# The second half's output weights converted behind the mixing operands of the first prefill blocks, in a hybrid attention and mLSTM step

## The chip, the cores and the metric

The kernel runs on one core of one Trainium2 chip. The metric is the device time of one execution in microseconds. The five engines are named as in the profile: PE (TensorE), DVE (VectorE), ACT (ScalarE), POOL (GpSimd) and SP (SyncE, which here only issues transfers).

## The reference

One layer of a diffusion backbone. An attention head group (8 query heads, 2 key heads, width 64) and a bidirectional mLSTM group (4 heads, width 128) read one input projection side by side; one output projection merges them, and a SwiGLU network follows. There are 128 context rows and 1024 latent rows of width 1024, in float32. The part that matters here:

```python
attn_o = attention(aq, keys, vals)
hm, st_f, st_b = mlstm_bidir(heads(mq), heads(mk) * (MLSTM_DK ** -0.5), heads(mv), gates, init_f, init_b)
hm = (hm.reshape(B, T, MLSTM_WIDTH) * jax.nn.sigmoid(mo)).astype(x.dtype)
mix = jnp.concatenate([attn_o, hm], axis=-1) @ w_out
x = x + g1 * mix
h2 = rmsnorm(x, norm2_w) * (1 + sc2) + sh2
x = x + g2 * swiglu(h2, w_gu, w_down)
```

## The kernel before

The rows are cut into nine blocks of 128 (block 0 is the context), and three blocks make a chunk. Every large product is done three times, so as to keep float32 precision: a matrix is split into a rounded part and the rest of it, and high by high, low by high and high by low are added in the same accumulator. So each weight piece, once loaded (`raw`, L162), is rounded by ACT (`whi`, L163) and its rest is taken by DVE (`wlo`, L141). A product of one row block with half of the output columns is 12 matmuls: four each on L1219, L1221 and L1223.

The order of work is not written out by hand. Python generators for the parts of the program are woven into each other, and a scheduler that keeps its own timeline then orders the instructions of each engine. `tc.issue_after(x)` and `behind(key)` put a floor under that: what is made inside stands behind instruction x, where it runs on x's engine. Every engine then runs its own list strictly in order. Memory comes from pools; a tile has a tag, and with `bufs=1` the next tile of the tag waits until the readers of the one before are done. A pool that opens later can lie on the memory of one that is closed.

The change is in the stretch from about 480 to 590 us, where the mLSTM scan ends and the output projection takes over. `attn_out_first` (L1320) has done the attention half of it for the first three blocks, using the tiles `gta` and `mxa` of the pool hTp; its parts `ada` make the gate rows of the last modulation, two half rows of 512, each one with a bias row from b_ada (L477), a product (L479), a sum (L480), a scaling (L482), and a store to the scratch tensor g_d by ACT's queue (L483). `prefill` (L1226) then does the mLSTM half for all nine blocks:

- `mix(b)` transposes a block's mLSTM rows `hmr` on PE (L120); ACT rounds them into the tile `mx` (L1265), DVE takes the rest (L141).
- `half(b, n)` is the 12 matmuls of block b with column half n; DVE multiplies by the gate (L1180, into a tile t2), POOL adds to the row (L1181).
- `end(b)` squares and sums a finished row on ACT (`jk`, L1398), with the reciprocal root on DVE (L131 to L137), and runs `norm2`: ACT scales the rows to `y` (L1414), PE transposes them, ACT and DVE shift them (`fl`, L1422 and L1424), and so the SwiGLU network gets its operands.

`out_pieces(1, n)` loads and splits the weights of the column half n for the mLSTM rows. Into all this the attention of the next chunk is woven: queries `qr` are loaded from q_d (L1078, ACT's queue), transposed (L120) and rounded (`qT`, L1089); then scores S (L1111), their maximum on DVE (L1113), exponentials on ACT (`pr`, `ph`), transposes by DMA on SP's queue (`phT`, `plT`), and the product with the values (`po`, L1135 and L1136).

Of the kernel before, what the change touches and what calls it, by code (L numbers as in the profile page):

```python
# [8 lines left out]
F32 = mybir.dt.float32  # L9
# [10 lines left out]
P = 128  # L20
# [26 lines left out]
def hybrid_step(ctx: ExitStack, tc: tile.TileContext, I: dict, O: dict):  # L47
# [92 lines left out]
    def sub(out, full, hi, eng):  # L140
        (dve if eng == "dve" else pool).tensor_tensor(out=out, in0=full, in1=hi, op=ALU.subtract)  # L141

# [131 lines left out]
    es1 = ExitStack()  # L274
    hTp = es1.enter_context(tc.tile_pool(name="hTp", bufs=1, reuse_waits="tile"))
    gp = es1.enter_context(tc.tile_pool(name="gp", bufs=1, reuse_waits="tile"))
# [144 lines left out]
    hp = ctx.enter_context(tc.tile_pool(name="hpk", bufs=1, side="right", reuse_waits="tile"))  # L421
    hT = [(hTp if c < 2 else rowp).tile([P, 2, KD, CT], F16, name=f"hT{c}", tag=f"hT{c}" if c < 2 else "b4") for c in range(NCH)]
    hTh, hTl = [t[:, 0] for t in hT], [t[:, 1] for t in hT]
# [752 lines left out]

    def add_gated(x1, ps, g, n, eng=dve):
        cs = slice(n * 512, (n + 1) * 512)
        t = t2()
        dve.tensor_tensor(out=t, in0=ps, in1=g, op=ALU.mult)  # L1180
        eng.tensor_tensor(out=x1[:, cs], in0=x1[:, cs], in1=t, op=ALU.add)  # L1181
# [44 lines left out]
    def prefill(cur, nxt):  # L1226
# [4 lines left out]
        def load_hm(b):  # L1231
            if b >= NB:
                return None
            hm = xe.tile([P, 512], F32, name=nm("hmr"), tag="hmr", bufs=2)
            if b < CB:
                loaded["hm"] = dma(hm, hm_d[0][b * P : (b + 1) * P, :]).ins
            else:
                r = dma(hm.rearrange("p (h n) -> p h n", n=P), hm_d[b // CB][:, :, b % CB * P : (b % CB + 1) * P])
                if b == CB:
                    loaded["hm"] = r.ins  # L1240
            return hm
# [9 lines left out]
        gate = loaded["gate"] = dma(gx_all, g_d[0, 0:1, :].to_broadcast([P, D])).ins  # L1251
        ws.append(out_pieces(1, 1))
        cur["gate"] = loaded["piece"]
        gx = [gx_all[:, n * 512 : (n + 1) * 512] for n in range(2)]
        mixed = {}

        def mix(b):
            t = xe.tile([P, NQ, P], F32R, name=nm("mx"), tag="mx", bufs=3)
            th, tl = mixed[b] = t[:, 0:4], t[:, 4:8]
            hm = hms.pop(0)  # L1260
            ps = bank()
            for j in range(4):
                transpose(ps[:, j * P : (j + 1) * P], hm[:, j * P : (j + 1) * P])
            psv = ps.rearrange("p (j x) -> p j x", j=4)
            nc.scalar.copy(th, psv)  # L1265
            sub(tl, psv, th.bitcast(F32), "dve")
            with tc.issue_after(gate):
                hms.append(load_hm(b + 2))

        def half(b, n):  # L1270
# [29 lines left out]
        yield  # L1300
        yield from end(0)
        load_x1(3)
# [3 lines left out]
        yield  # L1306
        yield from end(1)
        for b in range(2, NB):
            load_x1(b + 2)
            half(b, 0)  # L1310
            yield
            if b + 1 < NB:
                mix(b + 1)
                yield
            half(b, 1)
            yield
            yield from end(b)

    def attn_out_first(oT, ready):


        x1 = rowp.tile([P, CB, D], F32, name="x1a", tag="b4")
        gt = hTp.tile([P, 6, 512], F32, name="gta", tag="hT1")
        mx = hTp.tile([P, CB, NQ, P], F32R, name="mxa", tag="hT0")
# [236 lines left out]
    for name, bufs in (("mm1", 1), ("po", 1)):  # L1561
        psum[name] = ctx.enter_context(tc.tile_pool(name="q" + name, bufs=bufs, space=PSUM, reuse_waits="tile"))
    homes["wq"] = ctx.enter_context(tc.tile_pool(name="wq", bufs=1, reuse_waits="tile"))
    xe = ctx.enter_context(tc.tile_pool(name="xe", bufs=1, reuse_waits="tile"))
    xg = ctx.enter_context(tc.tile_pool(name="xg", bufs=1, reuse_waits="tile"))
# [116 lines left out]
```

## Time and profile before

| | us |
|---|---|
| median of 3 runs | 1529.1 |
| the runs | 1527.36, 1529.1, 1534.01 |
| the profiled execution | 1531.07 |
| its span, first to last instruction | 1529.3 |
| PE busy | 1473.0 (96%) |
| DVE busy | 1015.8 (66%) |
| ACT busy | 770.4 (50%) |
| POOL busy | 268.8 (18%) |
| mean granted TensorE clock | 0.989 |

A row of the timeline has start, duration, engine, line, operation, output and inputs, shapes, the count of instructions taken together, and in brackets the idle time of the engine before it and what ended that. ACTq and SPq are the queues that issue transfers. Matmuls are pipelined, so a group's duration reaches over the start of the next.

### The profile page before, as it was taken

To read this page: it belongs to the slowest core of one execution; us is meant where nothing else is said; L and a number is where in the kernel's file an instruction comes from. 1 tells how busy PE (TensorE), PEld (TensorE's weight loads), DVE (VectorE), ACT (ScalarE), POOL (GpSimd) and SP (SyncE) were. 2 spreads that over 40 slices of the span, in tenths; PEclk is the share of its full clock that TensorE was granted. 3 is DMA by queue.
4 is the path that set the end of the run, shared out by engine and by line. 5 is a ranking of instruction groups with operands and counts; after the bars stand their busy time and mean duration, and the time that the engine had idled before them with its cause. 6 is when DMAs were issued, how large, how long until landed. Compare 5 with 4: busy or idle time off the path is not lost.

```text
span 1529.3 us, 23410 instructions
## 1 busy us (share of the span) xinstructions
PE 1473.0 (96%) x8539; PEld 1244.7 (81%) x8539; DVE 1015.8 (66%) x2025; ACT 770.4 (50%) x1429; POOL 268.8 (18%) x354
## 2 busy tenths in 40 slices
PE   6899999999998899999999999999999999999997
PEld 3545567677766789999898999989998989999996
DVE  4887654838568866878637587787866585554554
ACT  4764475947654645556433444656553443323333
POOL 0113423333344441010010100100010101101110
PEclk9899999999999999999999999999999999999998
DMA  9664323523456577869635357886864445544541
GB/s 359 205 198 147 101 71 42 120 53 62 110 177 207 135 180 187 200 156 195 171 115 166 124 184 212 198 184 145 201 145 138 138 139 179 158 135 126 153 144 56
DMA packets 387113, 233.77 MB, mean 153 GB/s; under 512 B 170102, under 2 KB 347462, under 8 KB 386998
## 3 DMA queue, kind: packets, MB, share of 16 engines
q1 hardware_dynamic: 385006, 228.69, 55.0%
q10 hardware_dynamic: 1864, 3.20, 0.9%
q8 instruction: 67, 1.10, 0.3%
q14 instruction: 48, 0.39, 0.1%
q0 software_dynamic: 128, 0.39, 0.1%
HBM read 182.21 MB, written 11.69 MB: 127 GB/s over the span
## 4 chain that ended last, share of the span: by engine, by line
PE 78%; DVE 5%; DMA 3%; ACT 3%; issue 1%; POOL 1%; SPq 0%; ACTq 0%; DVEq 0%; POOLq 0%
PE mm L1437 11%; PE mm L1436 11%; PE mm L1435 11%; PE mm L1191 5%; PE mm L1192 5%; PE mm L1193 5%; PE S L1111 4%; PE wi L514 3%; PE wi L513 3%; PE wi L512 3%; PE mm L1219 2%; PE po L1136 2%; PE po L1135 2%; PE mm L1221 2%; PE mm L1223 2%
## 5 line engine op out<-in xcount | busy, mean ns | idle before, releaser
L163 ACT CAST whi<-raw 128x1024 fp32r<-128x1024 f32 x214 | 219.2, 1026 | 367.8 <-PE mm L1436 146.9
L141 DVE TENSOR_TENSOR wlo<-raw,whi 128x1024 fp32r<-128x1024 f32 x214 | 257.7, 1204 | 170.5 <-ACT whi L163 167.0
L1436 PE MATMUL mm<-aTl,whi 128*128 128x384 f32 x1056 | 354.4, 336 | 0.0
L1437 PE MATMUL mm<-aTh,wlo 128*128 128x384 f32 x1056 | 354.2, 336 | 0.0
L1435 PE MATMUL mm<-aTh,whi 128*128 128x384 f32 x1056 | 353.2, 335 | 0.0
L141 POOL TENSOR_TENSOR hl<-tn,hl 128x384 fp32r<-128x384 f32 x66 | 84.9, 1286 | 846.6 <-ACT hl L1458 796.4
L1435 PEld LDWEIGHTS mm<-aTh,whi 128*128 128x128 f32 x1056 | 198.3, 188 | 0.7
L1436 PEld LDWEIGHTS mm<-aTl,whi 128*128 128x128 f32 x1056 | 198.3, 188 | 0.6
L1437 PEld LDWEIGHTS mm<-aTh,wlo 128*128 128x128 f32 x1056 | 198.3, 188 | 0.1
L1191 PE MATMUL mm<-whi,hl 128*128 128x512 f32 x372 | 144.4, 392 | 1.1 <-DVE t L1180 1.1
L1192 PE MATMUL mm<-wlo,hl 128*128 128x512 f32 x372 | 145.1, 391 | 0.0
L1193 PE MATMUL mm<-whi,hl 128*128 128x512 f32 x372 | 142.7, 391 | 0.0
L1118 DVE SCALAR_TENSOR_TENSOR pl<-pr,st,ph 128x1152 f16<-128x1152 f32 (+1 forms) x72 | 96.9, 1346 | 37.3 <-ACT ph L1117 35.9
L1113 DVE TENSOR_REDUCE st<-S 128x1 f32<-128x1152 f32 (+1 forms) x72 | 88.9, 1234 | 17.5 <-PE S L1111 17.2
L1114 ACT ACTIVATE pr<-S,st 128x1152 f32<-128x1152 f32 (+1 forms) x72 | 81.3, 1129 | 33.0 <-DVE st L1113 28.2
L1117 ACT ACTIVATE ph<-pr,st 128x1152 f16<-128x1152 f32 (+1 forms) x72 | 83.8, 1164 | 26.3 <-issue 10.9
L1180 DVE TENSOR_TENSOR t<-mm,gl 128x512 f32<-128x512 f32 x102 | 69.1, 686 | 38.1 <-PE mm L1193 16.0
L512 PE MATMUL wi<-headw,hT 128*128 128x384 f16 x288 | 93.9, 326 | 0.2 <-ACT th L799 0.2
L513 PE MATMUL wi<-headw,hT 128*128 128x384 f16 x288 | 93.9, 326 | 0.0
L514 PE MATMUL wi<-headw,hT 128*128 128x384 f16 x288 | 93.9, 326 | 0.0
L1111 PE MATMUL S<-kst,qT 128*128 128x384 f32 (+1 forms) x400 | 84.5, 344 | 0.8 <-ACT pr L1114 0.8
L1191 PEld LDWEIGHTS mm<-whi,hl 128*128 128x128 f32 x372 | 69.9, 188 | 15.2 <-DVE t L1180 1.5
(400 smaller groups left out, 2591.3 us busy)
## 6 DMA issues: line engine op xcount, KB each, us to landing
raw<-in_w_gu_dram SPq DMA_DIRECT2D x132, 512.0 KB
raw<-in_w_down_dram SPq DMA_DIRECT2D x60, 512.0 KB
a<-in_w_ada_dram SPq DMA_DIRECT2D x24, 512.0 KB
gl<-g_d SPq DMA_DIRECT2D x36, 256.0 KB
aw<-in_w_ada_dram SPq DMA_DIRECT2D x16, 512.0 KB
iraw<-in_w_in_dram SPq DMA_DIRECT2D x32, 256.0 KB
x<-in_x_sample_dram SPq DMA_DIRECT2D x11, 512.0 KB
raw<-in_w_out_dram SPq DMA_DIRECT2D x10, 512.0 KB
```

What stands on the lines that cost most here:

```text
L141: (dve if eng == "dve" else pool).tensor_tensor(out=out, in0=full, in1=hi, op=ALU.subtract)
L163: nc.scalar.copy(hi[:, :n], raw[:, :n])
L512: mm(ps[:, :n], ah, wh[:, k % 2, c0 : c0 + n], start=(k == 0), stop=False)
L513: mm(ps[:, :n], ah, wl[:, k % 2, c0 : c0 + n], start=False, stop=False)
L514: mm(ps[:, :n], al, wh[:, k % 2, c0 : c0 + n], start=False, stop=(k == KD - 1))
L1111: mm(S[:, n, 0:w], qT[:, h, :], kst[kv][:, t, c0 + n * w : c0 + (n + 1) * w], start=(t == 0), stop=(t == 1))
L1191: mm(ps, ah, wh[:, k % 2, :], start=(k == 0), stop=False)
L1192: mm(ps, ah, wl[:, k % 2, :], start=False, stop=False)
L1193: mm(ps, al, wh[:, k % 2, :], start=False, stop=(k == nk - 1))
L1435: mm(ps, wh[:, k, :], th[:, k, :], start=(k == 0), stop=False)
L1436: mm(ps, wh[:, k, :], tl[:, k, :], start=False, stop=False)
L1437: mm(ps, wl[:, k, :], th[:, k, :], start=False, stop=(k == KD - 1))
```

## The change

1. `out_pieces(1, 1)`, the second column half's weights, is made after `mix(0)` and `mix(1)`, with a floor: its rounding on ACT and its subtraction on DVE stand behind those of block 1's mixing operands. The first two blocks are mixed in one go.
2. The pool of `gta` and `mxa` is split in two, and `hmr` gets a pool of its own (xh, opened ahead of xe), so that the mixing tiles lie on other memory.
3. The loads of `hmr` for blocks 2 and 3 are issued behind the load of the gate rows, after the two mixes; `norm2` of a block comes one half later, behind `half(b + 3, 0)`.
4. The products with the gate of blocks 0 and 1 go into the attention's buffers "pr", not into the three t2 tiles.
5. The second bias row of the gate goes into the attention's tile "qr", not into `hmx`.

```diff
-    hTp = es1.enter_context(tc.tile_pool(name="hTp", bufs=1, reuse_waits="tile"))
+    hTp = [es1.enter_context(tc.tile_pool(name=f"hTp{c}", bufs=1, reuse_waits="tile")) for c in (1, 0)][::-1]
...
-            hm = xe.tile([P, 512], F32, name=nm("hmr"), tag="hmr", bufs=2)
+            hm = xh.tile([P, 512], F32, name=nm("hmr"), tag="hmr", bufs=2)
...
         gate = loaded["gate"] = dma(gx_all, g_d[0, 0:1, :].to_broadcast([P, D])).ins
-        ws.append(out_pieces(1, 1))
-        cur["gate"] = loaded["piece"]
...
-            nc.scalar.copy(th, psv)
-            sub(tl, psv, th.bitcast(F32), "dve")
-            with tc.issue_after(gate):
-                hms.append(load_hm(b + 2))
+            loaded["mx"] = nc.scalar.copy(th, psv).ins
+            loaded["ml"] = sub(tl, psv, th.bitcast(F32), "dve").ins
+            if b > 1:
+                with tc.issue_after(gate):
+                    hms.append(load_hm(b + 2))
...
-                add_gated(x1s[c][i], ps, g, n, pool)
+                if b < 2:
+                    if b == 0:
+                        mixed["t", n] = ap2.tile([P, 3, CT], F32, name=nm("t2"), tag="pr", bufs=2).rearrange("p a n -> p (a n)")
+                    t = mixed["t", n][:, b * 512 : (b + 1) * 512]
+                else:
+                    t = None
+                add_gated(x1s[c][i], ps, g, n, pool, t)
...
-            if 2 <= b < CB + 2:
-                yield from norm2(0, cur, b - 2)
 
         for b in range(2):
             mix(b)
+        with behind("mx"), behind("ml"):
+            ws.append(out_pieces(1, 1))
+        cur["gate"] = loaded["piece"]
+        with tc.issue_after(gate):
+            hms.extend([load_hm(2), load_hm(3)])
+        for b in range(2):
             yield
...
             half(b, 0)
             yield
+            if 3 <= b < CB + 3:
+                yield from norm2(0, cur, b - 3)
...
+        rows_at = [lambda: hmx[0:2, 512:1024],
+                   lambda: ap.tile([P, NQ, HD], F32, name="bias", tag="qr", bufs=1).rearrange("p h d -> p (h d)")[0:2]]
...
-                       lambda: hmx[:, 0:512], lambda: hmx[0:2, 512:1024], 1, store=nc.scalar.dma_start)
+                       lambda: hmx[:, 0:512], lambda: rows_at.pop(0)(), 1, store=nc.scalar.dma_start)
```

No engine gets more or fewer instructions. ACT's list at the start of prefill, before: the names mx_1239 and mx_1242 are the mixing operands of blocks 0 and 1, whi_1237 is the second piece of the second half's weights, g_d the stored gate row.

```order
L1265 CAST mx_1239_6285<-mm_1240_6286 128x512
L163 CAST whi_1237_6280<-raw_1236_6279 128x1024
L483 DMA g_d_81<-hmx_5720 2x512
L952 ACTIVATE jkh_1215_6180,ssh_1100_5629<-hm_1099_5628 128x128
L1265 CAST mx_1242_6295<-mm_1243_6296 128x512
L1089 CAST qT_1248_6323<-mm_1249_6324 64x4x128
L1078 DMA qr_1427_7265<-q_d4_73 128x512
L949 ACTIVATE hm_1099_5628<-nu_1216_6183,dn_1220_6194 128x128
L1089 CAST qT_1248_6323<-mm_1249_6324 64x4x128
L952 ACTIVATE jkh_1221_6200,ssh_1100_5629<-hm_1099_5628 128x128
L1265 CAST mx_1260_6385<-mm_1261_6386 128x512
L1114 ACTIVATE pr_1265_6397,st_1268_6400<-S_1269_6401,st_1268_6400 128x1152
```

And after, where whi_1238 and whi_1241 are the second half's weights, mx_1233 and mx_1235 the operands of blocks 0 and 1, and q_d3 the queries of attention block 3:

```order
L1263 CAST mx_1233_6281<-mm_1234_6282 128x512
L952 ACTIVATE jkh_1215_6184,ssh_1100_5632<-hm_1099_5631 128x128
L483 DMA g_d_81<-bias_6115 2x512
L949 ACTIVATE hm_1099_5631<-nu_1216_6187,dn_1220_6198 128x128
L1078 DMA qr_1247_6329<-q_d3_72 128x512
L952 ACTIVATE jkh_1221_6204,ssh_1100_5632<-hm_1099_5631 128x128
L1263 CAST mx_1235_6289<-mm_1236_6290 128x512
L163 CAST whi_1238_6298<-raw_1237_6297 128x1024
L163 CAST whi_1241_6304<-raw_1240_6303 128x1024
L1089 CAST qT_1248_6331<-mm_1249_6332 64x4x128
L1078 DMA qr_1425_7271<-q_d4_73 128x512
```

Both pieces of the second half's weights now stand behind the operands of block 1, and the load of q_d3, which before was issued near 345 us, stands between the g_d store and these.

PE's list behind half(0, 0), before: mm_1250 is half(1, 0), mm_1252 is half(0, 1), and qr the attention's queries.

```order
L1223 MATMUL mm_1245_6305<-whi_1226_6224,mx_1239_6285 128x512 x2
L1223 MATMUL mm_1245_6305<-whi_1228_6229,mx_1239_6285 128x512 x2
L120 MATMUL mm_1249_6324<-ident_85,qr_1247_6321 128x128 x4
L1219 MATMUL mm_1250_6333<-whi_1226_6224,mx_1242_6295 128x512 x2
L1219 MATMUL mm_1250_6333<-whi_1228_6229,mx_1242_6295 128x512 x2
L1221 MATMUL mm_1250_6333<-wlo_1227_6225,mx_1242_6295 128x512 x2
L1221 MATMUL mm_1250_6333<-wlo_1229_6230,mx_1242_6295 128x512 x2
L1223 MATMUL mm_1250_6333<-whi_1226_6224,mx_1242_6295 128x512 x2
L1223 MATMUL mm_1250_6333<-whi_1228_6229,mx_1242_6295 128x512 x2
L1219 MATMUL mm_1252_6349<-whi_1234_6274,mx_1239_6285 128x512 x2
L1219 MATMUL mm_1252_6349<-whi_1237_6280,mx_1239_6285 128x512 x2
```

After, mm_1251 is half(0, 1) and mm_1250 is half(1, 0):

```order
L1223 MATMUL mm_1245_6313<-whi_1226_6228,mx_1233_6281 128x512 x2
L1223 MATMUL mm_1245_6313<-whi_1228_6233,mx_1233_6281 128x512 x2
L1219 MATMUL mm_1251_6356<-whi_1238_6298,mx_1233_6281 128x512 x2
L120 MATMUL mm_1249_6332<-ident_85,qr_1247_6329 128x128 x4
L1219 MATMUL mm_1250_6341<-whi_1226_6228,mx_1235_6289 128x512 x2
L1219 MATMUL mm_1250_6341<-whi_1228_6233,mx_1235_6289 128x512 x2
L1221 MATMUL mm_1250_6341<-wlo_1227_6229,mx_1235_6289 128x512 x2
L1221 MATMUL mm_1250_6341<-wlo_1229_6234,mx_1235_6289 128x512 x2
L1223 MATMUL mm_1250_6341<-whi_1226_6228,mx_1235_6289 128x512 x2
L1223 MATMUL mm_1250_6341<-whi_1228_6233,mx_1235_6289 128x512 x2
L120 MATMUL mm_1260_6393<-ident_85,hmr_1243_6309 128x128 x4
```

The first two matmuls on the second half's weights have moved ahead of the query transposes and of half(1, 0).

ACT's list where the first rows are normed, before: jk_1291 is the square of block 2, y the rows of block 0.

```order
L1398 ACTIVATE jk_1273_6433,s1_1272_6432<-x1a_5709 128x1024
L1114 ACTIVATE pr_1283_6478,st_1286_6481<-S_1287_6482,st_1286_6481 128x1152
L1117 ACTIVATE ph_1284_6479<-pr_1283_6478,st_1286_6481 128x1152
L1398 ACTIVATE jk_1291_6514,s1_1290_6513<-x1a_5709 128x1024
L1414 ACTIVATE y_1299_6535<-x1a_5709,ry_1257_6369 128x512
L1414 ACTIVATE y_1301_6548<-x1a_5709,ry_1257_6369 128x512
L1422 ACTIVATE fl_1298_6534<-mm_1300_6537,shift2_90,scale2_89 128x128
```

After, jk_1289 is the square of block 2:

```order
L1114 ACTIVATE pr_1281_6484,st_1284_6487<-S_1285_6488,st_1284_6487 128x1152
L1117 ACTIVATE ph_1282_6485<-pr_1281_6484,st_1284_6487 128x1152
L1427 ACTIVATE y_1299_6558<-x1a_5712,ry_1256_6376 128x512
L1427 ACTIVATE y_1308_6592<-x1a_5712,ry_1256_6376 128x512
L1411 ACTIVATE jk_1289_6520,s1_1288_6519<-x1a_5712 128x1024
L1435 ACTIVATE fl_1298_6557<-mm_1300_6560,shift2_90,scale2_89 128x128
L1263 CAST mx_1310_6605<-mm_1311_6606 128x512
```

The two y now stand ahead of that square.

More of the change, by code (lines that the diff above doesn't have):

```diff
@@ L140, in sub @@
     def sub(out, full, hi, eng):
-        (dve if eng == "dve" else pool).tensor_tensor(out=out, in0=full, in1=hi, op=ALU.subtract)
+        return (dve if eng == "dve" else pool).tensor_tensor(out=out, in0=full, in1=hi, op=ALU.subtract)
     loaded = {"n": 0}
@@ L421, in hybrid_step @@
     hp = ctx.enter_context(tc.tile_pool(name="hpk", bufs=1, side="right", reuse_waits="tile"))
-    hT = [(hTp if c < 2 else rowp).tile([P, 2, KD, CT], F16, name=f"hT{c}", tag=f"hT{c}" if c < 2 else "b4") for c in range(NCH)]
+    hT = [(hTp[c] if c < 2 else rowp).tile([P, 2, KD, CT], F16, name=f"hT{c}", tag=f"hT{c}" if c < 2 else "b4") for c in range(NCH)]
     hTh, hTl = [t[:, 0] for t in hT], [t[:, 1] for t in hT]
@@ L1175, in t2, with add_gated @@
         return ft.tile([P, 512], F32, name=nm("t2"), tag="t2", bufs=3)
-    def add_gated(x1, ps, g, n, eng=dve):
+    def add_gated(x1, ps, g, n, eng=dve, t=None):
         cs = slice(n * 512, (n + 1) * 512)
-        t = t2()
+        t = t2() if t is None else t
         dve.tensor_tensor(out=t, in0=ps, in1=g, op=ALU.mult)
@@ L1300, in prefill @@
         yield
-        yield from end(0)
+        end(0)
         load_x1(3)
@@ L1306, in prefill @@
         yield
-        yield from end(1)
+        end(1)
         for b in range(2, NB):
@@ L1316, in prefill @@
             yield
-            yield from end(b)
+            end(b)
     def attn_out_first(oT, ready):
         x1 = rowp.tile([P, CB, D], F32, name="x1a", tag="b4")
-        gt = hTp.tile([P, 6, 512], F32, name="gta", tag="hT1")
-        mx = hTp.tile([P, CB, NQ, P], F32R, name="mxa", tag="hT0")
+        gt = hTp[1].tile([P, 6, 512], F32, name="gta", tag="hT1")
+        mx = hTp[0].tile([P, CB, NQ, P], F32R, name="mxa", tag="hT0")
         ip = [wp.tile([P, 1024], F32, name=nm("ip"), tag=f"ipair{i // 2}", bufs=2) for i in range(4)]
@@ L1563, in hybrid_step @@
     homes["wq"] = ctx.enter_context(tc.tile_pool(name="wq", bufs=1, reuse_waits="tile"))
+    xh = ctx.enter_context(tc.tile_pool(name="xh", bufs=1, reuse_waits="tile"))
     xe = ctx.enter_context(tc.tile_pool(name="xe", bufs=1, reuse_waits="tile"))
```

## The prediction

> **What bounds the kernel now.** I began with the page's busy times and the sums by stage.
>
> ```profile
> PE 1473.0 (96%) x8539; PEld 1244.7 (81%) x8539; DVE 1015.8 (66%) x2025; ACT 770.4 (50%) x1429; POOL 268.8 (18%) x354
> 485.00:530.00 45.00, 38.99 (x180) 31.18 (x179) 37.83 (x99) 24.89 (x43) 19.52 (x15) 0.92 0.66 181
> 530.00:600.00 70.00, 69.56 (x402) 62.04 (x400) 46.98 (x73) 34.76 (x51) 23.32 (x17) 1.00 0.69 178
> ```
>
> PE (TensorE) is the bound. After each window's length come the busy times of PE, its weight loads, DVE, ACT and POOL, then the granted clock, the DMA share and GB/s. In the stage that the change rewrites, 485 to 530 us, PE stands idle for 6.01 of 45 us and the clock averages 0.92; in the 70 us behind it the idle time is 0.44. Nothing can be won except idle PE and slow PE, and both lie in the first window. Next, PE's waits from 485 to 600 us summed by releaser, of which the first and the last are shown, and from PE's timeline the rows that waited, with the gap and its releaser in brackets:
>
> ```profile
> PE mm L120 <- ACT y L1414: 1.8, 1, 1.8
> ...
> PE po L1135 <- DMA phT<-ph: 0.4, 1, 0.4
> 488.60 1.19 PE L1219 MATMUL mm<-whi,mx 128*128 128x512 f32 x4 [1.81 <-ACT mx L1265]
> 491.92 0.60 PE L120 MATMUL mm<-ident,qr 128*128 128x128 f32 x4
> 501.12 1.20 PE L1219 MATMUL mm<-whi,mx 128*128 128x512 f32 x4 [1.61 <-DVE mx L141]
> 517.17 1.55 PE L120 MATMUL mm<-ident,y 128*128 128x128 f32 x8 [1.82 <-ACT y L1414]
> 520.15 2.04 PE L1219 MATMUL mm<-whi,mx 128*128 128x512 f32 x4 [0.57 <-DVE fl L1424]
> ...
> 525.16 1.21 PE L1111 MATMUL S<-kst,qT 128*128 128x384 f32 x6
> ```
>
> Four gaps make 1.81 + 1.61 + 1.82 + 0.57 = 5.81 us. The slow part is the block at 520.15. Its twelve matmuls take 525.16 - 520.15 = 5.01 us. The one at 488.60 took 491.92 - 488.60 = 3.32 us with four transposes among them (0.60 us by their row, less where they overlap), so some 2.8 alone. The clock by windows says why:
>
> ```profile
> 500.00:510.00 10.00, 8.88 (x42) 7.53 (x43) 8.73 (x13) 5.02 (x8) 7.15 (x4) 1.00 0.98 256
> 516.00:518.00 2.00, 0.83 (x6) 0.63 (x7) 2.00 (x5) 1.87 (x5) 0.33 (x1) 1.00 0.99 120
> 518.00:520.00 2.00, 1.57 (x8) 1.17 (x6) 2.00 (x7) 1.17 (x3) 0.94 (x1) 0.51 0.87 180
> 520.00:522.00 2.00, 1.85 (x5) 1.50 (x6) 1.97 (x11) 2.00 (x5) 0.00 (x0) 0.50 0.32 95
> 522.00:524.00 2.00, 2.00 (x6) 1.61 (x5) 0.61 (x4) 2.00 (x5) 0.79 (x1) 0.50 0.16 48
> 524.00:525.00 1.00, 1.00 (x4) 0.76 (x4) 0.00 (x0) 0.81 (x1) 1.00 (x2) 0.57 0.00 0
> ```
>
> From 518 to past 524 us the granted clock is half. At half clock 1.57 + 1.85 + 2.00 us of busy PE, and 0.43/0.5 of the last microsecond, do half the work: (5.42 + 0.86)/2 = 3.1 us lost. With the 0.57 gap, then, 518 to 525 loses 3.7. So there are 5.8 + 3.1 = 8.9 us to win here at most.
>
> **The change, part by part.** ACT and DVE are in-order, so what counts is who stands behind whom:
>
> ```profile
> 466.81 0.25 ACTq L483 DMA_DIRECT2D g_d<-hmx  x1
> 468.77 0.27 SPq L477 DMA_DIRECT2D hmx<-in_b_ada_dram  x1
> 486.21 1.04 ACT L163 CAST whi<-raw 128x1024 fp32r<-128x1024 f32 x1 [1.95 <-DMA raw<-in_w_out_dram]
> 486.89 0.17 DVE L947 RECIPROCAL dn<-dn 128x2 f32<-128x2 f32 x1
> 487.58 1.20 DVE L141 TENSOR_TENSOR wlo<-raw,whi 128x1024 fp32r<-128x1024 f32 x1
> 487.67 0.40 ACT L949 ACTIVATE hm<-nu,dn 128x128 f32<-128x128 f32 x1
> 487.96 0.58 ACT L1265 CAST mx<-mm 128x512 fp32r<-128x512 f32 x1
> 488.71 0.41 DVE L482 TENSOR_SCALAR hmx<-hmx 2x512 f32<-2x512 f32 x1
> 489.75 0.31 ACT L952 ACTIVATE jkh<-hm 128x128 bf16<-128x128 f32 x1 [0.26 <-DVE hm L950]
> 499.11 1.36 DVE L1113 TENSOR_REDUCE st<-S 128x1 f32<-128x1152 f32 x1 [1.47 <-PE S L1111]
> 500.39 0.68 DVE L141 TENSOR_TENSOR mx<-mm,mx 128x512 fp32r<-128x512 f32 x1
> 515.37 1.04 ACT L1398 ACTIVATE jk<-x1a 128x1024 bf16<-128x1024 f32 x1
> 516.41 1.32 ACT L1414 ACTIVATE y<-x1a,ry 128x512 f32<-128x512 f32 x2
> ```
>
> First gap, 1.81 us. The w_out cast at 486.21 leaves the path. The mixing cast then follows the reciprocal, which ends at 487.06, through hm (0.40) and itself (0.58): 488.04 in place of 488.54 to 488.60. **Gain 0.55**, not 1.04, because DVE's chain becomes late in its stead. The split of the pools adds nothing to it: the cast begins right behind hm, not behind a release of memory.
>
> Second gap, 1.61 us. The mixing subtraction of block 2 stood behind the 1.36 us softmax maximum; now it stands ahead of it, and PE has half(1,1) to do, whose operands are long there. **Gain 1.61.** It costs 0 as long as the weights' subtractions are done by then; were they late, the same 1.6 would come back.
>
> Third gap, 1.82 us. The y rows of block 0 now stand ahead of the 1.04 us square (jk) of block 2. **Gain 1.04**; 0.78 stays. Fourth gap, 0.57: half(3,1) is now behind the norm's transposes and has its own inputs early. **Gain 0.57.** Since norm2 comes one half later, a wait for a mixing cast may appear near 529 us: 0 to 1, bounded by the 1.82 that the worst such wait cost, **0.5 taken**.
>
> Together: 0.55 + 1.61 + 1.04 + 0.57 - 0.5 = 3.27.
>
> Now the new wait. The second bias row takes the tile "qr", so the attention queries of block 3 can't be loaded until the g_d store has read it; the load is ACT's own and stands in ACT's queue ahead of jkh, block 1's mixing cast and both w_out casts. None of this is in the trace of before, so I bound it. A store of the same size on the same queue was issued at 466.81 and let SP go on at 468.77: 1.96 us. The slow end, 4.53, is a 256 KB store in a crowded stretch of the chain of waits; a 256 KB load, the size of qr, stands beside it:
>
> ```profile
> 561.91 2.06 DMA t<-in_x_sample_dram
> 564.00 4.53 DMA x_d<-t
> SPq L477 <- DMA g_d<-hmx: 1.6, 1, 1.6
> 466.80:468.80 2.00, 2.00 (x14) 1.74 (x13) 0.87 (x3) 1.39 (x3) 0.00 (x0) 1.00 0.73 237
> 488.40:490.40 2.00, 1.80 (x8) 1.50 (x9) 2.00 (x6) 1.50 (x4) 0.17 (x1) 1.00 0.84 253
> 492.57 0.37 ACTq L1078 DMA_DIRECT2D qr<-q_d  x1
> ```
>
> Short end: the row is ready near 488.2, L482 no longer being behind the 1.20 us subtraction of 487.58, and ACT issues the store after its mixing cast and jkh, near 488.45; it lands at 490.41; the load's issue (0.37) ends at 490.78, jkh at 491.09, the cast at 491.67, the first w_out cast (1.04) at 492.71. PE ends half(0,0) at 488.05 + 3.32 = 491.37: a gap of 1.34. PE then has two matmuls (half of the 1.19 us that four take at 488.60, so some 0.5) before the query transposes, and the load lands at 490.78 + 2.06 = 492.84, in time. Long end, 4.53 for both: store 492.98, first cast 495.28, gap 3.9; load at 497.9, PE ready at 495.8, 2.1 more; together 6.0. Below zero is excluded: before, PE had work there without a gap. I take **1.7**, near the short end, because its row has the same store and a DMA share of 0.73 against 0.84 here: 0.84/0.73 of 1.96 is 2.26, 0.3 later. So 3.27 - 1.7 = 1.6 us net of idle time.
>
> The clock. The dip follows the 1.82 gap and the half-idle window 516 to 518 (0.83 busy of 2.00). With 0.78 left there, I take the dip as gone: **3.1**. The gaps of 1.81 and 1.61 brought no dip: the clock is 1.00 from 488.40 to 490.40 and from 500 to 510 above; so a gap of 1.7 need not bring one either. The Trainium skill, "TensorE: Matmul & The Clock Gate", section "Part 1: The HAM clock gate", has the clock halve after an idle window of about 3.4 us, a window that runs freely; this trace has a dip at a gap of 1.82 us, so the measurement decides that less than 3.4 us of pure idleness is enough, and what the page adds is that the phase may matter, which would move this term between 0 and 3.1 from run to run.
>
> Loads: the two w_gu pieces that SP issued at 488.81 follow later, ahead of their casts. The bias load sits in a quiet stretch of SP. POOL has the same adds. Instruction counts don't change. All these cost nothing while PE's own work covers them; past 530 us PE waits 0.44 in 70, so that cover is thin at one place, told below.
>
> Sum: 1.6 + 3.1 = 4.7. The profiled execution took 1531.07 us, 1.8 beyond its span of 1529.3, and lies 2.0 above the median of 1529.1: 1531.07 - 4.7 = 1526.4.
>
> **The rivals.**
>
> The ACT wait decides (slower side). Place: the qr load behind the g_d store, with the first w_out cast behind both. At the long ends the gap is 6.0; a gap that long, against 1.82 that did it once, brings its own dip. Then 3.27 - 6.0 + 3.1 - 3.1 = -2.7: 1533.8. It ends above the profiled run once the gap passes 3.3 us with a dip. For it: the DMA engines are 0.84 busy there. Against: the same store took 1.96 at 0.73. If the dip of 518 us stays as well, 1533.8 + 3.1 = 1536.9.
>
> The dip doesn't go, or appears at another gap: 1.6 alone, 1529.5. For it: one gap of 1.8 made it and two of 1.8 and 1.6 didn't, so the size alone does not decide.
>
> The time is given back at 580 us. The page's chain ends there in DMA, not in PE:
>
> ```profile
> 568.92 5.19 DMA raw<-in_w_gu_dram
> 574.11 5.78 DMA phT<-ph
> ```
>
> PE waited 0.44 for that phT. It starts from PE's own last halves and so should come earlier with them, but at the DMA share of the 570s it may not by the whole 4.7; 2 to 4 come back: 1529.4.
>
> More than forecast: no new wait shows, since the store lands early, and every gap goes: 5.8 + 3.1 = 8.9 at most, 1522.2; from the lowest run (1527.36) rather than the profiled one, less still.
>
> **How the numbers follow.** Forecast 1526.4: chance 0.42, with its own range 1524 to 1528.5. The dip stays: 0.18. Given back at 580: 0.12. The ACT wait with a dip: 0.18, of which a quarter reaches 1536 and beyond. More than forecast: 0.10. The range 1521 to 1535 leaves out the far ends of the first and the last. About half a per cent, 7.6 us, is what a measurement of this kernel tells from no change: faster needs under 1521.5, and takes the best end of "more" and of fast runs, 0.12; slower needs over 1536.7, 0.13, as other mishaps in so crowded a queue can't be excluded; the same, 0.75.
>
> **What would show it.** Right: the first L1219 of the stage at 488.0 to 488.2; then a gap of 1.4 to 2.2 before the first matmul on the second half's weights, put down to ACT's whi; no gap at half(1,1); under 1 at y; clock 1.00 from 515 to 526; the first gate_up matmul some 4 to 5 us earlier. Wrong: a gap over 3.3 at 491 us, query transposes waiting for a DMA, a half clock anywhere from 490 to 535, or a wait of over 1 us for phT near 575.

## The result, and the profile after

The changed kernel took 1533.57 us (median of 17 runs, 1530.57 to 1538.09) and the kernel before 1530.5 us beside it (17 runs, 1525.87 to 1534.23). The ratio is 1.0022, with a 95% interval of 1.0012 to 1.0032: slower by 1.8 to 4.9 us, where 4.7 us less was forecast. The profiled execution took 1534.34 us, with a span of 1532.5.

First the page's busy times and the two stages of the changed kernel, in the columns of the prediction's first rows; then PE's waits from 485 to 600 us:

```profile
PE 1474.5 (96%) x8539; PEld 1247.0 (81%) x8539; DVE 1018.1 (66%) x2025; ACT 770.2 (50%) x1429; POOL 270.1 (18%) x354
485.00:530.00 45.00, 39.35 (x193) 31.53 (x192) 36.95 (x97) 24.27 (x43) 19.05 (x17) 0.96 0.65 189
530.00:600.00 70.00, 67.04 (x378) 60.19 (x376) 47.38 (x72) 34.10 (x49) 25.31 (x16) 0.98 0.72 177
PE po L1135 <- DMA phT<-ph: 2.4, 1, 2.4
PE mm L120 <- ACT y L1427: 2.0, 1, 2.0
PE mm L1219 <- DVE mx L141: 1.8, 1, 1.8
PE mm L1219 <- ACT mx L1263: 1.8, 2, 1.2
PE mm L120 <- DMA qr<-q_d: 0.5, 1, 0.5
```

PE's idle time is 45 - 39.35 = 5.65 us in the stage that was rewritten (6.01 before) and 70 - 67.04 = 2.96 in the 70 us behind it (0.44 before). The first stage won 0.4 us, and the second gave 2.5 back. The rows of PE's timeline that carry these waits:

```profile
490.21 1.20 PE L1219 MATMUL mm<-whi,mx 128*128 128x512 f32 x4 [1.23 <-ACT mx L1263]
495.52 0.71 PE L1219 MATMUL mm<-whi,mx 128*128 128x512 f32 x2 [1.82 <-DVE mx L141]
496.76 0.66 PE L120 MATMUL mm<-ident,qr 128*128 128x128 f32 x4 [0.53 <-DMA qr<-q_d]
519.53 1.12 PE L120 MATMUL mm<-ident,y 128*128 128x128 f32 x4 [1.96 <-ACT y L1427]
536.38 1.19 PE L1219 MATMUL mm<-whi,mx 128*128 128x512 f32 x4 [0.56 <-ACT mx L1263]
580.90 0.36 PE L1135 MATMUL po<-phT,vs 128*128 128x256 f16 x1 [2.39 <-DMA phT<-ph]
```

The times carry an offset. The scores of the attention (L1111) are a mark that every run has; the same group of them, at about 400 us and at about 600, starts in the kernel before (first and third row) and after (second and fourth) at:

```profile
400.30 1.36 PE L1111 MATMUL S<-kst,qT 128*128 128x384 f32 x6
401.89 1.36 PE L1111 MATMUL S<-kst,qT 128*128 128x384 f32 x6
597.52 1.21 PE L1111 MATMUL S<-kst,qT 128*128 128x384 f32 x6
601.77 1.21 PE L1111 MATMUL S<-kst,qT 128*128 128x384 f32 x6
```

The 1.59 us at 400 arise before any changed instruction has run: the offset is the same from the first such mark at 165 us on. Between 400 and 600 us the changed kernel loses 4.25 - 1.59 = 2.66 us, of which 1532.5 - 1529.3 - 1.59 = 1.6 are left at the end of the program. In the forecast it would have won 4.7 there.

### The profile page after: what moved, and what is told of

The parts are those of the page before. It is cut to its first block, busy times and chain, and to the rows that moved or that the text cites. A ratio compares the mean times of both kernels' runs of the same rounds, so it can differ in the third digit from the quotient of the medians.

```text
span 1532.5 us, 23401 instructions
## 1 busy us (share of the span) xinstructions
PE 1474.5 (96%) x8539; PEld 1247.0 (81%) x8539; DVE 1018.1 (66%) x2025; ACT 770.2 (50%) x1429; POOL 270.1 (18%) x354
## 4 chain that ended last, share of the span: by engine, by line
PE 79%; DVE 6%; ACT 3%; DMA 2%; issue 1%; POOL 1%; SPq 0%; ACTq 0%; DVEq 0%; POOLq 0%
PE mm L1450 12%; PE mm L1449 12%; PE mm L1448 12%; PE mm L1191 5%; PE mm L1192 5%; PE mm L1193 5%; PE S L1111 4%; PE wi L514 3%; PE wi L513 3%; PE wi L512 3%; PE po L1135 2%; PE po L1136 2%; PE mm L1219 2%; PE mm L1221 1%; PE mm L1223 1%
## 5 line engine op out<-in xcount | busy, mean ns | idle before, releaser
L1113 DVE TENSOR_REDUCE st<-S 128x1 f32<-128x1152 f32 (+1 forms) x72 | 88.9, 1235 | 15.5 <-PE S L1111 15.1
L1111 PE MATMUL S<-kst,qT 128*128 128x384 f32 (+1 forms) x400 | 84.3, 344 | 0.8 <-ACT pr L1114 0.8
```

What stands on the lines that cost most here:

```text
L1111: mm(S[:, n, 0:w], qT[:, h, :], kst[kv][:, t, c0 + n * w : c0 + (n + 1) * w], start=(t == 0), stop=(t == 1))
```

## The experiments

Each kernel was profiled and, but for one, timed in five rounds beside the kernel before; ratios are to that. The expectations speak of theories by letter: A is the new wait on ACT as the cause, D the transfers and SP's order ahead of the first phT at 580 us, E the reciprocal roots on DVE that became late; for any other letter the text itself says what is expected.

**The wait on ACT (A).** u5 is the changed kernel with part 5 undone: the second bias row goes into `hmx` again, and the load of qr waits for nothing.

```diff
-                   lambda: ap.tile([P, NQ, HD], F32, name="bias", tag="qr", bufs=1).rearrange("p h d -> p (h d)")[0:2]]
+                   lambda: hmx[0:2, 512:1024]]
```

> The second bias row is back in hmx, so the load of the queries is not held by the g_d store. Theory A (the loss is ACT's new wait at 491 to 497 us, gaps of 1.82 and 0.53 us): both gaps go, the phT wait at 580 us shrinks with the bunching, and the time falls by 2.3 to 3 us, to 1530.5 to 1531.3. Theory B (the loss is at 580 us, where the attention's ph stands behind a w_gu cast whose transfer lands late): the two gaps go, but phT is still waited for by 2 us or more, and since PE only arrives earlier at the same transfer, the time falls by 0 to 1.5, to 1532 to 1533.6.

Measured: 1.0026 [1.0014, 1.0037], 1536.44 us. In PE's timeline both gaps at 495 us are gone, and the one at y has grown:

```profile
523.31 1.12 PE L120 MATMUL mm<-ident,y 128*128 128x128 f32 x4 [6.61 <-ACT y L1427]
```

Taking A's 2.35 us (1.82 + 0.53) away doesn't make the kernel faster, but this edit doesn't price A either: the gap at y grew by 6.61 - 1.96 = 4.65 us. In this run ACT waited for the last step of the root (L137), which ended at about 522.5. That A alone isn't the cause is shown better by kp, below: it keeps both gaps (1.54 and 0.87) and is no slower than the kernel before.

**The parts, undone and alone.** u1 takes `out_pieces(1, 1)` ahead of the mixes again (part 1 undone), u3 puts norm2 back to its old place, u4 gives blocks 0 and 1 the t2 tiles again. o1 is the kernel before with part 1 alone (with the loads of `hmr` behind it), o3 with the later norm2 alone; their edits are those rows of the change.

```diff
 u1
         gate = loaded["gate"] = dma(gx_all, g_d[0, 0:1, :].to_broadcast([P, D])).ins
+        ws.append(out_pieces(1, 1))
+        cur["gate"] = loaded["piece"]
...
-        with behind("mx"), behind("ml"):
-            ws.append(out_pieces(1, 1))
-        cur["gate"] = loaded["piece"]
 u3
-            if 3 <= b < CB + 3:
-                yield from norm2(0, cur, b - 3)
...
+            if 2 <= b < CB + 2:
+                yield from norm2(0, cur, b - 2)
 u4
-                if b < 2:
+                if False:
```

> The second half's weights are made ahead of the mixes again, as before the change; the other four parts stay. If moving the weights is worth what it was made for, this is slower than after by 0.5 (the first gap, 1.8 again in place of 1.2) and faster by what the weights wait behind the mixing operands (1.82): a net -1.3, 1532.3, with theory A. With theory B the wait at 580 us stays at 2 us or more and the net is within 1 us of 1533.6.

> norm2 at its old place (behind the second half of block b + 2, not behind the first half of block b + 3); all else as after. If the later norm is what delays the attention's chain and so phT (a form of theory B), the phT wait falls under 1 us and the time by 1.5 to 3 us, to 1530.5 to 1532. Theory A, and theory B with the cast alone as its cause: phT still waits 2 us or more, 1533 to 1534.5.

> The changed kernel with part 4 undone: the gated products of blocks 0 and 1 go through the three t2 buffers again. If the three buffers were a bound in this stretch, half(2, 0) waits for POOL's adds, a gap of 1 to 2 us shows on PE there, and the ratio to before is 1.003 to 1.004. If they were not, the ratio stays at the 1.0022 of the changed kernel, give or take what a reordered list brings.

> The kernel before, with part 1 alone (the second half's weights behind the mixing operands, the loads of hmr behind both mixes). The queries are loaded near 345 us as before, so no transfer stands in ACT's list here. By the forecast's sum the first gap gives 0.55 and half(0, 1) waits some 0.5 for the weights: a ratio of 0.9985 to 1.0000. Theory C: SP's list has the w_gu piece behind the last x load here too, so phT is waited for by 1.5 us or more: 1.0000 to 1.0020.

> The kernel before, with part 3's later norm alone (norm2 one half later), nothing else of the change. SP's list then has the fourth w_gu piece behind the last x load, as after. Theory C: phT is waited for by 1.5 us or more at 580, and the ratio is 1.0005 to 1.0020 by that alone. If the loss needs the other parts (PE arriving earlier), phT is waited for by less than 1 us and the ratio is 0.9990 to 1.0005.

Measured: u1 1.0035 [1.0023, 1.0047], u3 1.0033 [1.0021, 1.0045], u4 1.0037 [1.0023, 1.0050], o1 1.0036 [1.0023, 1.0049], o3 1.0012 [0.9999, 1.0026]. No part that was taken out makes the kernel faster, and neither of the two tried alone gains; u1, u3, o1, and u5 above, came out slower than any theory in their expectations gave. In each of them another wait shows; from PE's timelines, u4's two (products with the gate at 506.74, as was expected of three t2 buffers, and block 3's mixing cast), o1's and o3's:

```profile
506.74 1.20 PE L1219 MATMUL mm<-whi,mx 128*128 128x512 f32 x4 [1.61 <-DVE t L1180]
540.03 1.41 PE L1219 MATMUL mm<-whi,mx 128*128 128x512 f32 x4 [4.11 <-ACT mx L1263]
522.24 1.97 PE L120 MATMUL mm<-ident,y 128*128 128x128 f32 x8 [4.32 <-ACT y L1419]
517.63 0.66 PE L120 MATMUL mm<-ident,y 128*128 128x128 f32 x4 [2.28 <-ACT y L1413]
```

Any of these edits lets the scheduler order the small steps anew, so an undo tells what the whole does without that part, not what the part costs. A wait of over 1 us for y shows in u4 (1.10), o1 and o3, and none in u1 and u3. What all five share is a wait of 1.8 to 2.8 us near 580 us. Part 2, the split pools, was not tried by itself.

**The roots on DVE (E).** A block's y needs the reciprocal root of its row sums: L131, L132, L133 and three Newton steps (the formula that refines a first guess) of L135, L136, L137, twelve instructions of 0.15 us each. These are rows of the changed kernel's timeline, from DVE, POOL and ACT in order of time, around block 0's root:

```profile
508.00 0.15 DVE L131 TENSOR_SCALAR rv<-s 128x1 f32<-128x1 f32 x1 [0.33 <-ACT jk L1411]
510.93 2.40 POOL L1181 TENSOR_TENSOR x1a<-x1a,t 128x512 f32<-128x512 f32 x1 [2.14 <-DVE t L1180]
512.09 1.25 DVE L135 TENSOR_TENSOR rt<-ry 128x1 f32<-128x1 f32 x1
513.33 1.34 DVE L1113 TENSOR_REDUCE st<-S 128x1 f32<-128x1152 f32 x1
516.08 1.28 POOL L1181 TENSOR_TENSOR x1a<-x1a,t 128x512 f32<-128x512 f32 x1 [2.75 <-DVE ry L137]
516.13 1.32 DVE L135 TENSOR_TENSOR rt<-ry 128x1 f32<-128x1 f32 x2
517.37 0.14 DVE L1116 TENSOR_SCALAR st<-st 128x1 f32<-128x1 f32 x1
517.61 0.23 DVE L137 SCALAR_TENSOR_TENSOR ry<-rt,ry 128x1 f32<-128x1 f32 x2
517.61 1.26 ACT L1117 ACTIVATE ph<-pr,st 128x1152 f16<-128x1152 f32 x1 [1.59 <-DVE rt L136]
518.77 1.32 ACT L1427 ACTIVATE y<-x1a,ry 128x512 f32<-128x512 f32 x2
```

The root takes from 508.00 to 517.84, because its steps stand between long instructions in DVE's list, and two of them, on one element a partition, took over 1.2 us. Both of these ended with an add on POOL that had begun first: 512.09 + 1.25 = 513.34 beside 510.93 + 2.40 = 513.33, and 516.13 + 1.32 = 517.45 (a group of two) beside 516.08 + 1.28 = 517.36. They hold up the softmax as well: the first its maximum (L1113), the second its scaling (L1116), and with them ph, behind which y stands on ACT. The root was ready at 517.61 + 0.23 = 517.84 and ph ended at 517.61 + 1.26 = 518.87, so what y waited for last was ph. In the kernel before the same y followed jk at once. One such long step stood ahead of the scaling there too, again ending with an add on POOL:

```profile
512.68 1.29 POOL L1181 TENSOR_TENSOR x1a<-x1a,t 128x512 f32<-128x512 f32 x1 [0.76 <-DVE rt L136]
512.72 1.26 DVE L137 SCALAR_TENSOR_TENSOR ry<-rt,ry 128x1 f32<-128x1 f32 x1
```

So what the changed kernel has more is the one at 512.09, some 1.1 us over its usual 0.15, about what the gap is over the forecast (1.96 - 0.78 = 1.18); this is an estimate from these rows, and no run takes that one step away. The Trainium skill, "SBUF — State Buffer", section "SBUF: two separate sides", has DVE and POOL share a port pair as an exclusive lock, which a DVE instruction with two SBUF inputs needs, so that the later of the two waits for the whole of the other; the ends above agree with it.

k2 is the changed kernel with one Newton step in place of three in the roots of the first three blocks; it leaves two steps of the computation out. bk2 is the kernel before with the same edit. kp leaves nothing out: the three steps of those roots go to POOL, four instructions each.

```diff
 k2, bk2
-        for _ in range(3):
+        for _ in range(steps):
...
-                    cur["rs"] += stats(x1s[0][b : b + 1])
+                    cur["rs"] += stats(x1s[0][b : b + 1], 1)
 kp
-        for _ in range(3):
+        for _ in range(3 if eng is not None else 0):
+            eng.tensor_tensor(out=t, in0=y, in1=y, op=ALU.mult)
+            eng.tensor_tensor(out=t, in0=t, in1=v, op=ALU.mult)
+            eng.tensor_scalar(out=t, in0=t, scalar1=-0.5, scalar2=1.5, op0=ALU.mult, op1=ALU.add)
+            eng.tensor_tensor(out=y, in0=y, in1=t, op=ALU.mult)
+        for _ in range(0 if eng is not None else 3):
...
-                    cur["rs"] += stats(x1s[0][b : b + 1])
+                    cur["rs"] += stats(x1s[0][b : b + 1], pool)
```

> The changed kernel with one Newton step in place of three in the reciprocal roots of the first three blocks' second norm (two are left out, so those rows are less exact): 18 small DVE instructions less between 508 and 530 us. If the gap ahead of the y transposes (1.96 us after, 0.78 forecast) is DVE's chain and not ACT's order, it falls under 0.8 us and the marks up to 564 us come 1.2 to 2 us earlier. Theories C and D: phT does not come earlier by as much, and most of this is waited for at 580, so the ratio stays above 1.0012. If PE's gaps alone set the time: 1.0008 to 1.0014.

> The kernel before the change, with one Newton step in place of three in the roots of the first three blocks' second norm (two are left out, as in k2). Theory E (the change put y ahead of the square on ACT, and so made DVE's root the last thing that y waits for; before, ACT's square was): here the gap ahead of y keeps 1 us or more, and the ratio is 0.9992 to 1.0002, less than half of the 0.0040 that k2 gained on after. If the root was as late in the kernel before, it gains as much here: 0.9955 to 0.9970.

> The changed kernel with the three Newton steps of those roots on POOL (four instructions a step there, for three on DVE); nothing is left out. Theory E: DVE's list no longer stands between the square and y; if POOL's small instructions take 0.1 to 0.3 us each, the root takes 2 to 4 us in place of 10, the gap of 1.96 falls under 0.8, and the time is near that of k2, ratio 0.9980 to 1.0000. If POOL's instructions come late behind the 1.3 us additions, the gap stays and the ratio is 1.0020 or more.

Measured: k2 0.9982 [0.9967, 0.9997], bk2 1.0009 [0.9996, 1.0021], kp 0.9988 [0.9977, 0.9999], 1530.41 against 1532.61 us. Taking the work away gains 0.0040 on the changed kernel, more than any theory in k2's expectation gave, and nothing on the kernel before; moving it to POOL gains 0.0034 on the changed kernel. PE's row at y in kp, ACT's rows of y and ph there, and PE's first two rows of y in bk2:

```profile
517.16 0.66 PE L120 MATMUL mm<-ident,y 128*128 128x128 f32 x4 [0.50 <-ACT y L1432]
516.38 1.34 ACT L1432 ACTIVATE y<-x1a,ry 128x512 f32<-128x512 f32 x2 [3.63 <-POOL ry L138]
519.40 1.26 ACT L1122 ACTIVATE ph<-pr,st 128x1152 f16<-128x1152 f32 x1
516.47 1.03 PE L120 MATMUL mm<-ident,y 128*128 128x128 f32 x8
520.79 0.65 PE L120 MATMUL mm<-ident,y 128*128 128x128 f32 x4 [2.85 <-ACT y L1414]
```

So of E one half is shown: in the changed kernel the late roots set the third gap; with their steps off DVE it falls to 0.50, and the kernel comes out 0.0012 below the kernel before in place of 0.0022 above it. They set it in part through the order of ACT's list, which follows them: in kp y stands ahead of ph, and waits for the root alone. What this is worth depends on the rest of the list: the same move to POOL gains 0.0034 on the changed kernel, but 1.0003 - 0.9989 = 0.0014 on f and 1.0016 - 0.9999 = 0.0017 on h3 (both below).

The other half of E, that the roots did not matter in the kernel before, is not shown. In bk2 the eight transposes of block 0's y come without any wait; the 2.85 us are at block 1's y. So the gap ahead of block 0 closes there too. The time does not fall, and its profile shows other waits in place of that gap: these 2.85 us, and 2.57 for phT near 580.

**The wait at 580 us (D).** In the changed kernel the chain that ended last passes, in order, a w_gu load, ph and the transposing transfer phT (first three rows); the kernel before's is in the prediction. SP's list differs there too: before, the third w_gu piece was issued ahead of the last x load of the stretch; now it stands behind it, and that load waits for a store. f takes ph ahead of the w_gu cast on ACT, h3 lets SP issue that piece ahead of the x load, h5 is h3 with a later w_gu piece behind ph and two gate loads behind plT.

```diff
 f
-                    act(phv, prv, AF.Copy, scale=st[:, 3:4])
+                    loaded["ph"] = act(phv, prv, AF.Copy, scale=st[:, 3:4]).ins
 f, h3 (h3: hot(2000) in place of behind("ph"), k == 3)
-                for _ in range(4):
-                    next(main)
+                for k in range(4):
+                    with behind("ph") if c == 0 and k > 2 else nullcontext():
+                        next(main)
 h5, besides
-        dma(gl, g_d[idx, 1:2, cs].to_broadcast([P, 512]))
+        with behind("plT") if c == 0 else nullcontext():
+            dma(gl, g_d[idx, 1:2, cs].to_broadcast([P, 512]))
...
```

> The changed kernel with one floor more: the fourth w_gu cast of the gate and up products stands behind the attention's ph, not ahead of it, on ACT; all else as after. Theory B: the phT wait of 2.39 us at 580 falls below 0.5 and the half clock behind it goes; 2 to 3.4 us saved, 1530.2 to 1531.6. Theory A: nothing or under 0.5 us, 1533.1 to 1533.6, as the gaps at 491 to 497 stay.

> The changed kernel with one load raised in the scheduler's priority: the fourth w_gu piece, so that SP issues it ahead of the last x load of prefill, and ACT's list has its cast ahead of pr and ph again, as both stood before the change. Theory C (SP holds that piece behind a load that waits for a store, so a burst of transfers starts some 3 us late and phT, last in it, lands as late as before although PE arrives earlier): phT lands 2 to 3 us earlier, PE waits under 1 us for it, and the time falls by 2 to 3 us, to a ratio near 1.0003 to 1.0010. Theory D (the amount that has to be moved ahead of phT sets its landing, whatever the order): phT lands where it did, 2 us or more of waiting stay, ratio 1.0018 to 1.0026.

> As h3, and the two gate rows of 256 KB that the down products use later (gl and gx) are loaded behind the transposes, so 0.5 MB less stands ahead of phT. Theory C: as h3, within 0.5 us. Theory D: at about 270 GB/s, 0.5 MB are 1.9 us, so phT lands that much earlier than in h3 and the wait shrinks by as much: ratio 0.0010 to 0.0015 under that of h3.

Measured: f 1.0003 [0.9993, 1.0014], h3 1.0016 [1.0004, 1.0028], h5 1.0109 [1.0086, 1.0132]. From the chains of the changed kernel (three rows) and of f (two), and the row in which SP issues phT in kp:

```profile
569.62 5.18 DMA raw<-in_w_gu_dram
575.84 1.26 ACT ph L1117
577.11 3.65 DMA phT<-ph
571.19 4.49 DMA raw<-in_w_gu_dram
575.67 6.74 DMA phT<-ph
575.64 1.49 SPq L1125 DMA_TRANSPOSE phT<-ph  x1
```

With the offsets at 400 us taken off (1.59 and 3.48), f issued phT 3.3 us earlier (572.19 against 575.52) and it took 6.74 us in place of 3.65: PE could go on at 579.07, against 579.31 in the changed kernel and 579.94 in the kernel before. In f, then, asking earlier hardly moved the landing. So time that PE wins before is waited off at this point: 0.44 us before, 2.39 after, 3.08 in f. The changed kernel came to it at 580.90 - 2.39 - 1.59 = 576.92, against 579.94 - 0.44 = 579.50 in the kernel before: of these 2.6 us, 0.6 passed. But the landing isn't fixed. In kp, whose offset is 2.19, phT was issued at 573.45 and PE went on at 577.31 (its row is below): 2.1 us earlier than in the changed kernel, and landed 2.0 earlier. What makes this transfer last 3.65 us in one run and 6.74 in another is not shown. h3's wait was 1.34 and its time came down by 0.0006 only, within the intervals, which neither C nor D had forecast. f timed 0.0019 lower than the changed kernel, though it waited longer. Its profile has no half clock from 485 to 600 us (the changed kernel's lost 3.4 us there, below), and between the marks it loses 602.00 - 597.52 - 3.48 = 1.00 us in place of 2.66; whether its twelve runs gained by the clock too can't be read from one profile. h5's list became worse elsewhere (waits for phT, plT and whi add up to 9 us behind 560 us), so it says nothing on the amount of transfers.

**The same kernel again, and both remedies together.** b2 is the kernel before, profiled once more, to see what two executions of one program differ by. kpf is kp with f's edit, h3kp is kp with h3's.

> The kernel before, unchanged, profiled once more. The profile of after is 1.60 us behind that of before already at 165 us, where both run the same list. If that is a difference between executions, this one is off by something between 0 and 3.5 us at that mark, as four variants were; if the change moved memory so that the start is slower, it is within 0.2 us of the first profile of before.

> The changed kernel with both remedies that gained singly: the Newton steps of the first three blocks' roots on POOL (0.9988 of before, 0.0034 below the changed kernel) and the last x load kept behind the cast ph on SP's list (1.0003, 0.0019 below the changed kernel). If the late roots on DVE and the late phT are two separate causes (E and D), the gains add: 1.0022 - 0.0034 - 0.0019 = 0.9969 of before, some 1527.8 where before is at 1532.6. If the wait for phT only swallows what comes early ahead of it (the landing is fixed by the transfers, not by the issue), the second adds nothing to the first: 0.9985 to 0.9990, and PE waits over 2 us for the first phT again.

> The changed kernel with the Newton steps on POOL and SP's list at 565 us as in the kernel before (the third w_gu piece ahead of the load that waits for an x store). If SP held by that load is what makes the first phT late (D as an order on SP), PE waits under 1.5 us for it instead of 2.7, and the time falls to 0.9980 to 0.9985 of before. If the landing is fixed by the amount of transfers, it stays at 2.5 and 0.9988. This list also moves other instructions behind 600 us, and a loss of 2 to 4 us there would give 1.000 to 1.001.

Measured: b2 1531.84 us; kpf 0.9989 [0.9978, 1.0000], h3kp 0.9999 [0.9988, 1.0010]. The two stages in b2, PE's rows at the wait in kp, kpf and h3kp, and the load in kpf's chain:

```profile
485.00:530.00 45.00, 38.49 (x194) 30.82 (x192) 39.29 (x99) 24.36 (x43) 21.40 (x17) 1.00 0.70 191
530.00:600.00 70.00, 68.85 (x395) 60.86 (x394) 47.13 (x74) 35.81 (x51) 22.93 (x17) 1.00 0.70 178
579.50 0.27 PE L1140 MATMUL po<-phT,vs 128*128 128x256 f16 x1 [2.74 <-DMA phT<-ph]
574.01 0.37 PE L1140 MATMUL po<-phT,vs 128*128 128x256 f16 x1 [2.30 <-DVE tn L1473]
573.29 0.45 PE L1453 MATMUL mm<-aTh,whi 128*128 128x384 f32 x1 [2.68 <-ACT whi L168]
563.25 7.29 DMA raw<-in_w_gu_dram
```

f's edit adds nothing to kp, and h3's shows no gain on it (0.9999 against 0.9988, with intervals that overlap). In all three PE loses 2.3 to 2.7 us at one place between 570 and 580 us; it goes by phT, by `tn` (behind a w_gu load of 7.29 us in the chain), or by the w_gu cast. The wait takes another name and stays. b2 shows the spread: its idle time in the two stages is 6.51 + 1.15 = 7.66, the kernel before's in the first profile 6.45, the changed kernel's 8.61; and b2's clock is 1.00 in both.

## Why the prediction was wrong, step by step

Of the sum, the largest error was the clock (3.1 us booked), the step whose failure an experiment shows is the third gap, and the wait at 580 us had been put into a rival and not into the sum. Of the signs of being wrong, three appeared: query transposes waiting for a DMA (0.53), a half clock at 520, and over 1 us of waiting for phT (2.39).

**First, second and fourth gap: right as gaps.** The first was 1.23 us against "1.81 - 0.55", so 1.26. But its matmul came no earlier: by the mark at 490.21 - 1.59 = 488.62, where it was 488.60 before and 488.0 to 488.2 was forecast, because PE had waited for `ip` twice just ahead (0.70 and 0.71 us, against 0.67 once; b2, the very program of before, waited 0.72 and 0.68). No gap shows at half(1,1) nor at the fourth place. The new wait for a mixing cast is 0.56 at 536 us, where 0.5 was taken near 529.

**The third gap: the step that failed.** "Gain 1.04; 0.78 stays" took the root as ready when jk begins. The gap is 1.96. What ended last was not the square on ACT but ph, at 518.87, held up by the root's steps on DVE; the root itself ended at 517.84. kp, whose edit moves just these steps, brings the gap to 0.50 and the kernel from 1.0022 to 0.9988. The mis-sized term is 1.96 - 0.78 = 1.2 us in the profile, and 0.0034, some 5 us, by the times, more than the gap itself. kp's and the changed kernel's profiles differ at the mark near 600 us by 3.2 (4.25 - 1.59 = 2.66 against 599.14 - 597.52 - 2.19 = -0.57), and of that 1.7 is one dip of the clock less (below). So a part of kp's gain isn't the gap, and what it is remains open.

**The new wait on ACT: the mechanism as told, 0.6 too small.** It was taken at 1.7, of the bounds 1.34 and 6.0; it measured 1.82 + 0.53 = 2.35. From ACT's timeline and the chain of the changed kernel:

```profile
490.45 2.63 DMA g_d<-bias
493.10 3.61 DMA qr<-q_d
493.50 0.31 ACT L952 ACTIVATE jkh<-hm 128x128 bf16<-128x128 f32 x1 [1.24 <-DMA g_d<-bias]
494.27 2.00 ACT L163 CAST whi<-raw 128x1024 fp32r<-128x1024 f32 x2
```

The profile puts the 1.82 down to DVE's `mx`; the matmuls that waited read the second half's weights, whose first cast, half of the 2.00 us, ended near 495.3, just ahead of them (495.52). The store took 2.63 us against the 1.96 that the forecast had from another store, the load 3.61 against 2.06. The store was estimated at 2.26 for the crowding; the load was not corrected for it.

**The clock: wrong.** The 3.1 us were to go with the third gap; the gap stayed, and so did a dip. Windows of the changed kernel, the granted clock third from the end:

```profile
520.00:522.00 2.00, 2.00 (x10) 1.90 (x9) 2.00 (x5) 1.94 (x5) 0.38 (x1) 0.50 0.87 148
522.00:524.00 2.00, 2.00 (x8) 1.57 (x8) 1.51 (x6) 1.84 (x4) 0.08 (x1) 0.77 0.31 94
580.00:582.00 2.00, 1.10 (x4) 1.13 (x5) 1.03 (x3) 0.00 (x0) 0.00 (x0) 0.74 0.82 218
582.00:584.00 2.00, 2.00 (x8) 2.00 (x8) 0.00 (x0) 0.79 (x1) 0.00 (x0) 0.50 1.27 274
```

Summed over windows of 1 us, the time lost to the half clock is 1.71 us at 520 and 1.71 at 581, together as much as the 3.42 of the kernel before at one place. Between 485 and 600 us it comes in multiples of 1.71 in the others too: none in b2, f and bk2, 1.71 in kp (at 496, not at y) and in kpf, 3.42 in k2 is 1.71 + 1.71, 5.1 in u5. Half a clock that costs 1.71 us lasts 3.4, which agrees with the window of the Trainium skill, "TensorE: Matmul & The Clock Gate", section "Part 1: The HAM clock gate". But b2 and the first profile are one program, with gaps that differ by little and dips of 0 and 3.42: the dip belongs to the execution as much as to the kernel. To book 3.1 us of one profile as a gain of the change was the largest error in the sum; its own rival ("the dip doesn't go") had less chance than it deserved.

**Given back at 580 us: the rival that came true.** It had a chance of 0.12 and "2 to 4 come back" under an otherwise right forecast. The wait for phT went from 0.44 to 2.39. The price was right, at its lower end; what was missed is that this wait is the rule and not an accident: PE lost 1.3 us or more at this stage in every variant here, though 0.44 and 0.83 in the two profiles of the kernel before. Of a gain ahead of it, a quarter passed in the changed kernel (0.6 of 2.6). Between the changed kernel and kp most did: kp came to it 2.35 us earlier (579.50 - 2.74 - 2.19 = 574.57 against 576.92), and 2.0 passed.

With what was measured, the sum in idle time is 0.58 + 1.61 - 0.14 + 0.57 - 0.56 - 2.35 - 1.95 = -2.2, and 6.45 against 8.61 in the stages is the same 2.2; against b2's 7.66 it is 0.95. The clock cancels between the two profiles. That is a loss of 1 to 2 us out of the 3.4 (1.8 to 4.9) of the times. The rest stays open: the start-up differs from run to run by up to 6.2 us (below), and a single profile of each can't say how often the dips come with either kernel.

The version that beats both is kp: 0.9988 of the kernel before, with an interval that ends at 0.9999, so about 1.8 us, only just clear of no change; kpf is level with it.

## What to carry to other kernels

A gap that is named after one engine's instruction has to be followed one releaser further, with the time at which each operand was ready, before an edit on the named engine is counted as a gain. A chain of tiny dependent instructions on an in-order engine costs what stands between them, not their sum: 12 times 0.15 us took 9.8 us here. And a gain ahead of a point where a transfer is waited for (580 us) should be counted only for what passes that point, which was 0.6 us of 2.6 here.

## What the hardware showed

Instructions of a Newton step on 128x1 elements took some 1.25 us on DVE when they began under an add on POOL, and 0.15 to 0.23 otherwise, as above. Not every small instruction was held up so: L131 took 0.15 at 508.00, while POOL's add of 507.49 (1.29 us) was under way.

Two executions of the same list of instructions differ before any of it can matter: the mark at 165 us lies between -1.8 us (k2) and +4.4 us (u4) from the first profile of the kernel before, +1.49 in b2 for the very same program, and the offset stays within 0.05 us up to 400 us. Profiles are therefore compared from a common mark, and differences of spans of 1 to 4 us are no evidence.

A gap need not bring a dip of the clock: the waits of 3.08 us in f and 6.61 in u5 were followed by none and by 5.1 us of loss, 2.39 in the changed kernel by 1.71.
